# A hybrid retention and mLSTM backbone on one core: the first sixteen parameter blocks without splits, four latent chunks side by side

## The chip, the cores and the metric

The kernel runs on one core of a Trainium2 chip. TensorE (PE) multiplies matrices out of SBUF into PSUM; VectorE (DVE), ScalarE (ACT) and GpSimd (POOL) work beside it, each in the order of its own queue, and SyncE (SP) issues the transfers. The metric is the device time of one execution in microseconds (us).

## The reference

Two layers work on 512 latent tokens and 256 context tokens, with 1024 channels. What matters here is how a layer begins:

```python
mod_x = jax.nn.silu(c) @ w_ada[l] + b_ada[l]          # shift, scale, gate for the latent tokens
mod_c = jax.nn.silu(c_ctx) @ w_ada[l] + b_ada[l]      # the same for the context tokens
hx = _rmsnorm(x, norm_w) * (1.0 + sc_x[:, None]) + sh_x[:, None]
hc = _rmsnorm(ctx, norm_w) * (1.0 + sc_c) + sh_c
u = jnp.einsum('bld,de->ble', h, w_in) + b_in         # h is hx or hc
rq, rk, rv, rz, mq, mk, mv, mo, mz, mg, gr, gm = jnp.split(u, idx, axis=-1)
```

Behind it come a retention branch (`rq`, `rk`, `rv`, gate `rz`; rotary embedding on the latent q and k), an mLSTM branch (with the token gates `mg`), their merge, and one output projection with a residual. Everything is in 32-bit floats.

## The kernel before

**Layout.** Activations lie with channels on partitions, in 8 blocks `kb` of 128 channels; the 768 tokens are columns, context first (`CTX`, 256), then latent (`LAT`, 512). They form 6 chunks of 128 tokens: 0 and 1 are context, 2 to 5 latent. The modulated input is kept as a rounded part `h_hi` and its remainder `h_lo`; weights are split the same way by `split` (a copy on ACT, a subtraction on DVE or POOL) into `wh` and `wl`. A product is three matmuls: high by high, low by high, high by low.

**Who sets the order.** The code is written as one program; a scheduler places the instructions of each engine in a fixed order when the kernel is built, and buffers are taken from pools. A tile that takes a buffer waits until the last reader of the tile before it in that buffer is done. For the matmul results of the projections there are two PSUM buffers with the tag "lat" and two with the tag "ctx" (`atile`), in turn; small results use four others (`btile`). `stage` gives six SBUF buffers in turn.

**How it begins.** The first 16 of 24 parameter blocks of layer 0 are needed at once: block `kb` is the shift of channel block `kb`, block `8 + kb` its scale, each a 1024 by 128 matrix of 512 KB. `ada_load` and `ada_first` take the pair of a `kb` together: for kb 0 to 4 the pair is split, and 16 matmuls run with the silu values `sils` (both token kinds, high and low) as the stationary operand and the blocks as moving operand; for kb 5 to 7 (`NATSET`) the pair is used unsplit in fp32. `ada_fold` copies the resulting row and turns it into columns with small matmuls, and `mod_store` adds the bias. `rstd_rows` computes the norm (matmuls `ms_in`, `ms_inb`; for the context `ms_inc`, `ms_incb`). `modulate` scales and shifts each `kb`.

**The value and gate weights.** `projvg` multiplies one chunk of 128 tokens by 288 columns: 256 of `rv` for two heads and 32 of the token gates. `rvg(n)` calls it and then adds the bias twice on DVE: the values (L906) and the gate columns into `gtok`, a part of the gate work space `gw` (L907). Chunks 2 to 5 come first, then the first q projection (`ret_qk`, latent and context columns in one loop, L216 and L218), then chunks 0 and 1, then the k projection. Chunk n takes a buffer of the tag "lat" if n is even and "ctx" if it is odd. `gates` starts when `gtok` holds all six chunks; it is a long series on DVE. `rope` turns q and k on DVE (L649 to L651) and POOL. The context's modulation (`start_ctx`, on POOL, ACT and DVE: L389, L390) goes on beside `rvg` and the q projection.

## Time and profile before

| | us |
|---|---|
| median of 3 runs | 2023.96 (2020.58 to 2024.38) |
| the profiled execution, its own time | 2026.36 |
| its span, first to last instruction | 2024.6 |
| PE busy | 1986.7 (98% of the span) |
| DVE busy | 1347.0 (67%) |
| ACT busy | 715.9 (35%) |
| POOL busy | 371.0 (18%) |

The span is 1.8 us shorter than the profiled execution's own time, which is 2.4 us above the median. Mean granted TensorE clock over the span: 0.991 of full speed. A busy share is a mean over stages with different limits; what ends a wait is read from the stage itself.

### The profile page before, as it was taken

How to read it: one execution, taken by the hardware profiler on the slowest of the kernel's cores; microseconds unless marked ns; L12 is line 12 of the kernel's file. 1: busy time of each engine (PE TensorE's matmuls, PEld its weight loads, DVE VectorE, ACT ScalarE, POOL GpSimd, SP SyncE). 2: the span in 40 equal slices, each digit the busy share in tenths (PEclk: the TensorE clock that was granted, in tenths of full speed). 3: DMA queues.
4: the chain of work that ended last, by engine and by line, in shares of the span. 5: the costliest groups of instructions: out<-in, count | busy, mean ns of one | idle time of the engine just before them, and what ended most of it. 6: DMA issues, size and time to landing. Idle time of an engine off the chain costs nothing.

```text
span 2024.6 us, 32087 instructions
## 1 busy us (share of the span) xinstructions
PE 1986.7 (98%) x12612; PEld 1795.0 (89%) x12612; DVE 1347.0 (67%) x2897; ACT 715.9 (35%) x1346; POOL 371.0 (18%) x431
## 2 busy tenths in 40 slices
PE   7999999999999999999999998999999999999997
PEld 6988989999999999888888888899899999988887
DVE  7886785566868585766334689655568886763456
ACT  5423322333434334343112442322334444434323
POOL 4312221311212121100000332222212212110000
PEclk8989999999999999999999999999999999999999
DMA  8213432122323223456323521222233333325435
GB/s 298 75 50 100 137 98 87 58 88 74 112 74 110 80 87 115 160 205 213 119 79 144 162 86 59 95 62 74 89 114 99 116 118 116 118 94 190 133 122 170
DMA packets 80471, 231.64 MB, mean 114 GB/s; under 512 B 9600, under 2 KB 18048, under 8 KB 79296
## 3 DMA queue, kind: packets, MB, share of 16 engines
q1 hardware_dynamic: 76224, 213.66, 32.3%
q0 software_dynamic: 4096, 15.93, 2.0%
q8 instruction: 99, 1.62, 0.3%
q14 instruction: 52, 0.43, 0.1%
HBM read 208.39 MB, written 21.17 MB: 113 GB/s over the span
## 4 chain that ended last, share of the span: by engine, by line
PE 89%; DVE 6%; issue 2%; DMA 2%; ACT 0%; POOL 0%; SPq 0%; POOLq 0%; DVEq 0%
PE mv L232 11%; PE mqk_l L216 9%; PE rqk_l L216 8%; PE rv L232 4%; PE bm_l L216 4%; PE br_l L216 4%; PE gr_l L216 4%; PE gm_l L216 4%; PE mz_l L216 4%; PE rz_l L216 4%; PE mqk_c L218 3%; PE rqk_c L218 3%; PE ou L205 2%; PE ro L741 2%; PE mo L867 2%
## 5 line engine op out<-in xcount | busy, mean ns | idle before, releaser
L232 PE MATMUL mv<-wh_vo,h_hi 128*128 128x256 f32 x640 | 183.6, 287 | 0.0
L232 PE MATMUL mv<-wl_vo,h_hi 128*128 128x256 f32 x640 | 183.2, 286 | 0.0
L232 PE MATMUL mv<-wh_vo,h_lo 128*128 128x256 f32 x640 | 182.0, 284 | 0.0
L232 PEld LDWEIGHTS mv<-wh_vo,h_hi 128*128 128x128 f32 x640 | 122.6, 191 | 0.4
L232 PEld LDWEIGHTS mv<-wh_vo,h_lo 128*128 128x128 f32 x640 | 122.5, 191 | 0.2
L232 PEld LDWEIGHTS mv<-wl_vo,h_hi 128*128 128x128 f32 x640 | 122.4, 191 | 0.0
L790 DVE SCALAR_TENSOR_TENSOR cv<-u,vec,cv 128x770 f32<-128x770 f32 (+1 forms) x128 | 121.2, 948 | 1.8
L820 POOL TENSOR_TENSOR ws<-ws,gw 128x768 f32<-128x768 f32 (+1 forms) x32 | 53.4, 1688 | 321.9 <-PE mo L869 155.6
L216 PE MATMUL mqk_l<-h_lo,wh_mqk 128*128 128x512 f32 x256 | 103.8, 406 | 0.0
L216 PE MATMUL mqk_l<-h_hi,wh_mqk 128*128 128x512 f32 x256 | 103.3, 404 | 0.0
L216 PE MATMUL mqk_l<-h_hi,wl_mqk 128*128 128x512 f32 x256 | 102.6, 401 | 0.0
L652 POOL TENSOR_TENSOR ws<-ws,rp 128x512 f32<-128x512 f32 x32 | 52.9, 1653 | 176.6 <-DVE ws L651 144.8
L232 PE MATMUL rv<-wl_rv,h_hi 128*128 128x256 f32 x288 | 83.5, 290 | 0.0
L232 PE MATMUL rv<-wh_rv,h_hi 128*128 128x256 f32 x288 | 83.5, 290 | 0.0
L232 PE MATMUL rv<-wh_rv,h_lo 128*128 128x256 f32 x288 | 83.1, 289 | 0.0
L349 DVE SCALAR_TENSOR_TENSOR adj<-gw 128x512 f32<-128x512 f32 x112 | 74.9, 698 | 7.9 <-DMA gw<-in_wadat 4.2
L205 PE MATMUL ou<-yh,wl_wout 128*128 128x256 f32 (+1 forms) x256 | 79.3, 311 | 0.4 <-DVE wl_wout L162 0.4
L205 PE MATMUL ou<-yl,wh_wout 128*128 128x256 f32 (+1 forms) x256 | 79.1, 310 | 0.0
L205 PE MATMUL ou<-yh,wh_wout 128*128 128x256 f32 (+1 forms) x256 | 78.8, 310 | 0.0
L693 POOL TENSOR_TENSOR ws<-ws,ws 128x768 f32<-128x768 f32 (+1 forms) x32 | 52.9, 1673 | 118.8 <-PE ro L741 118.6
L741 PE MATMUL ro<-ws,ws 128*128 128x128 f32 x448 | 65.7, 279 | 7.7 <-DVE st L742 5.4
L741 PEld LDWEIGHTS ro<-ws,ws 128*128 128x128 f32 x448 | 60.1, 194 | 10.9 <-DVE st L742 6.1
(441 smaller groups left out, 6475.2 us busy)
## 6 DMA issues: line engine op xcount, KB each, us to landing
gw<-in_wadat SPq DMA_DIRECT2D x64, 256.0 KB, 3.5
raw_vo<-in_wblk SPq DMA_DIRECT2D x32, 512.0 KB, 4.0
raw_mqk<-in_wblk SPq DMA_DIRECT2D x32, 512.0 KB, 3.9
raw_wout<-in_wout SPq DMA_DIRECT2D x32, 512.0 KB, 3.6
gw<-grow SPq DMA_DIRECT2D x8, 1536.0 KB, 6.2
raw_qk<-in_wblk SPq DMA_DIRECT2D x16, 512.0 KB, 3.4
raw_zq<-in_wblk SPq DMA_DIRECT2D x16, 512.0 KB, 3.4
raw_kz<-in_wblk SPq DMA_DIRECT2D x16, 512.0 KB, 3.5
```

The costliest lines, as they stand in the source:

```text
L205: pe.matmul(dst, lw[:, j, kb], mv[:, kb, sl], start=first, stop=last)
L216: pe.matmul(lat, lw[:, j, kb], mv[:, kb, LAT], start=first, stop=last)
L218: pe.matmul(c[:, :NCTX], lw[:, j, kb], mv[:, kb, CTX], start=first, stop=last)
L232: pe.matmul(dst, sx[:, kb, tk], mv[:, :, kb], start=first, stop=last)
L349: v.scalar_tensor_tensor(junk, bufs[n % 4], 1.0, rows[:, d], op0=OP.mult, op1=OP.mult, accum_out=(part if q else m)[:, d:d + 1])
L652: g.tensor_tensor(dst[:, LAT], dst[:, LAT], t[:, :512], op=OP.add)
L693: g.tensor_tensor(chunks(qd[d][:, qsl], nq), chunks(qT[:, qsl], nq), xi[d][:, None, :].to_broadcast([P, nq, P]), op=OP.mult)
L741: pe.matmul(o, lt, rt, start=k == 0, stop=k == len(ops) - 1)
L790: v.scalar_tensor_tensor(y[:, o0:o0 + n], u[:, o0 + i:o0 + i + n], cw[i], y[:, o0:o0 + n], op0=OP.mult, op1=OP.add)
L820: g.tensor_tensor(qd[d][:, qsl], qT[:, qsl], gw[:, 2 + d, qsl], op=OP.mult)
L867: pe.matmul(o, ch(sT[d], n), vt[:, n, 0:129], start=True, stop=first)
```

## The change

The first sixteen blocks are no longer split. Shift blocks 1, 3, 4, 6 and 7 (`BYROW`) are loaded from the transposed copy of the parameters and multiplied on DVE by a row of silu values (`ada_shift`: two products of 512 columns with a running sum, then one small add), once for the latent tokens (d=0) and once for the context tokens (d=1). The other eleven blocks are the stationary operand of eight fp32 matmuls whose moving operand `sil` has two columns (`ada_first`), so that the result stands in columns at once. The rows of silu values are made by PE from the identity (`sil_row`) and lie in the start-up part of the gate work space `gw`. POOL scales `xin` by the norm in place, all eight `kb` before the first modulation. `projvg` takes several chunks and goes through them within each `kb`; for the latent ones the parameter and modulation steps of a `kb` are issued ahead of its matmuls (`start_lat`). The adds of `rvg` stand behind the matmuls of all four chunks. The first q and k projections do their latent columns one after the other, then come chunks 0 and 1, then the context columns of q and k. The weights for q and k are loaded in `start_lat`, no longer by `nextw`.

```diff
-        early = big.tile([P, 6, KB, P], F32, tag="b4", name="early")
+        xin = big.tile([P, KB, T], F32, tag="b2", name="xin")
+        shift = big.tile([P, 6, KB * P], F32, tag="b3", name="shift")
+        scale = big.tile([P, 6, KB, P], F32, tag="b4", name="scale")
         gw0 = gat.tile([P, 4, T], F32, tag="gw", name="gw_start").rearrange("p a b -> p (a b)").rearrange(
-            "p (a k c) -> p a k c", a=3, k=KB)
+            "p (a k) -> p a k", a=3)
+        srows, BYROW = gw0[:, 1:3], (1, 3, 4, 6, 7)
+        ring = [shift[:, 5]] + [scale[:, k].rearrange("p k c -> p (k c)") for k in range(6)] + [gw0[:, 0]]
+        ablk, acount = {}, [0]
 
         def ada_dma(kb):
-            r = []
-            for j, blk in enumerate((8 + kb, kb)):
-                k = (2 * kb + j) % 9
-                r.append(early[:, k] if k < 6 else gw0[:, k - 6])
-                nc.sync.dma_start(r[j], io["wada"][0, blk])
-            return r
-        raws = {0: ada_dma(0)}
-        xin = big.tile([P, KB, T], F32, tag="b2", name="xin")
+            for blk in (kb, 8 + kb):
+                if blk in BYROW:
+                    ablk[blk] = shift[:, BYROW.index(blk)]
+                    nc.sync.dma_start(ablk[blk], io["wadat"][0, blk])
+                else:
+                    ablk[blk] = ring[acount[0] % 8].rearrange("p (k c) -> p k c", k=KB)
+                    acount[0] += 1
+                    nc.sync.dma_start(ablk[blk], io["wada"][0, blk])
+        ada_dma(0)
         for kb in range(KB):
             nc.sync.dma_start(xin[:, kb, LAT], io["xT"][kb][:, LAT])
...
-        def projvg(w, hp, n, name):
-            ps = atile(("lat", "ctx")[n % 2], name)
...
+            pss = [atile(("lat", "ctx")[n % 2], f"{name}_{n}") for n in ns]
...
+                each(kb)
+                for ps, n in zip(pss, ns):
+                    for sx, mv in ((hp[0], w[0]), (hp[1], w[0]), (hp[0], w[1])):
+                        pe.matmul(ps[:, :VG], sx[:, kb, n * P:(n + 1) * P], mv[:, kb],
+                                  start=kb == 0 and sx is hp[0] and mv is w[0], stop=kb == KB - 1 and mv is w[1])
+            return pss
...
+        def sil_row(d):
+            for a in range(0, KB, 4):
+                ps = btile(f"silb{d}_{a}")
+                for k in range(4):
+                    pe.matmul(ch(ps, k), sil[:, a + k, d:d + 1].to_broadcast([P, P]), ident, start=True, stop=True)
+                s.activation(srows[:, d, a * P:(a + 4) * P], ps, AF.Copy)
+        spart = cst.tile([P, KB, 2, 2], F32, name="spart")
+        v.memset(spart, 0.0)
...
-        def ada_first(kb):
-            w = loaded["a", kb]
-            ps = btile(f"ada_{kb}")
-            if kb in NATSET:
-                for j in range(2):
-                    for k in range(KB):
-                        pe.matmul(ps[:, j * P:(j + 1) * P], sils[:, k].bitcast(F32), w[j][:, k], start=k == 0,
-                                  stop=k == KB - 1)
-            else:
-                for mv in w:
-                    for k in range(KB):
-                        pe.matmul(ps[:, :2 * P], sils[:, k], mv[:, :, k], start=k == 0 and mv is w[0],
-                                  stop=k == KB - 1 and mv is w[1])
-            return ps
-
-        def ada_fold(kb, ps):
-            row = stage(f"arow{kb}")[:4, :2 * P]
-            s.activation(row, ps[:4, :2 * P], AF.Copy)
-            pt = btile(f"adat_{kb}")
-            for j in range(2):
-                pe.matmul(pt[:, 2 * j:2 * j + 2], row[:, j * P:(j + 1) * P], fold, start=True, stop=True)
-            mod_store(0, 8 + kb, pt[:, 0:2])
-            mod_store(0, kb, pt[:, 2:4])
+        def ada_shift(kb, d):
+            junk, m = stage(f"adj0_{kb}_{d}"), mods[0][:, kb, d:d + 1]
+            for i in range(2):
+                w = ablk[kb][:, i * 512:(i + 1) * 512]
+                v.scalar_tensor_tensor(junk[:, :512], w, 1.0, srows[:, d, i * 512:(i + 1) * 512], op0=OP.mult, op1=OP.mult,
+                                       accum_out=spart[:, kb, d, i:i + 1])
+            v.scalar_tensor_tensor(m, spart[:, kb, d, 0:1], vec[0][:, V_BA + kb:V_BA + kb + 1], spart[:, kb, d, 1:2],
+                                   op0=OP.add, op1=OP.add)
+
+        def ada_first(blk):
+            ps = btile(f"ada_{blk}")
+            for k in range(KB):
+                pe.matmul(ps[:, 0:2], ablk[blk][:, k], sil[:, k], start=k == 0, stop=k == KB - 1)
+            mod_store(0, blk, ps[:, 0:2])
...
-        def modulate(l, x, rst, hp, sl, kb):
+        def modulate(l, x, rst, hp, sl, kb, scaled=False):
             m, d = mods[l], 1 if sl.start == 0 else 0
-            t = stage(f"xn{l}_{kb}_{d}")
-            g.tensor_tensor(t[:, sl], x[:, kb, sl], rst[:, sl], op=OP.mult)
+            if scaled:
+                t = x[:, kb]
+            else:
+                t = stage(f"xn{l}_{kb}_{d}")
+                g.tensor_tensor(t[:, sl], x[:, kb, sl], rst[:, sl], op=OP.mult)
...
-        ada_load(0)
-        rows = {0: ada_first(0)}
+        for kb in range(1, 4):
+            ada_dma(kb)
+        ada_first(0)
+        ada_first(8)
+        sil_row(0)
         for kb in range(KB):
             square_add(acc, xin[:, kb], kb, LAT)
-        ada_fold(0, rows[0])
-        ada_load(1)
         rstd_rows(acc, rst, LAT, "ms_in")
-        ada_load(2)
-        for kb in range(KB + 1):
-            if 0 < kb < KB:
-                rows[kb] = ada_first(kb)
-            ada_load(kb + 3)
-            if kb > 1:
-                ada_fold(kb - 1, rows[kb - 1])
-            if kb:
-                modulate(0, xin, rst, hp, LAT, kb - 1)
-            if kb == 3:
-                wload(0)
         for kb in range(KB):
-            nc.sync.dma_start(xin[:, kb, CTX], io["xT"][kb][:, CTX])
+            g.tensor_tensor(xin[:, kb, LAT], xin[:, kb, LAT], rst[:, LAT], op=OP.mult)
+
+        def start_lat():
+            for kb in range(KB):
+                if kb:
+                    if kb in BYROW:
+                        ada_shift(kb, 0)
+                    else:
+                        ada_first(kb)
+                    ada_first(8 + kb)
+                modulate(0, xin, rst, hp, LAT, kb, True)
+                if kb == 0:
+                    sil_row(1)
+                if kb + 4 < KB:
+                    ada_dma(kb + 4)
+                if kb == 3:
+                    wload(1)
+                    for k in range(KB):
+                        nc.sync.dma_start(xin[:, k, CTX], io["xT"][k][:, CTX])
+                yield
 
         def start_ctx():
             for kb in range(KB):
                 square_add(acc, xin[:, kb], kb, CTX)
             rstd_rows(acc, rst, CTX, "ms_inc")
             for kb in range(KB):
+                if kb in BYROW:
+                    ada_shift(kb, 1)
                 modulate(0, xin, rst, hp, CTX, kb)
                 if kb % 3 == 2:
                     yield
...
-            def ret_qk(w, blk, h, j):
+            def ret_qk(w, blk, h, j, only=None):
                 dst, vb, ctx = ((qTs[h % 2], V_RQ, need), (kTs[h % 2], V_RK, True))[j]
                 b = vc[:, vb + h:vb + h + 1]
-                pss = proj(w, blk, hp, ctx, f"rqk{l}_{h}_{j}")
-                rope(pss[0][0], b, dst, f"rp{l}_{h}_{j}")
-                if ctx:
-                    s.activation(dst[:, CTX], pss[1][0], AF.Identity, bias=b)
+                if only is None:
+                    pss = proj(w, blk, hp, ctx, f"rqk{l}_{h}_{j}")
+                elif only is CTX and not ctx:
+                    return
+                else:
+                    ps = atile("ctx" if only is CTX else "lat", f"rqk{l}_{h}_{j}_{only.start}")[:, :only.stop - only.start]
+                    mm3(ps, w[0], w[1], hp[0], hp[1], only, blk)
+                    pss = [(ps, only)]
+                for ps, sl in pss:
+                    if sl is LAT:
+                        rope(ps, b, dst, f"rp{l}_{h}_{j}")
+                    else:
+                        s.activation(dst[:, CTX], ps, AF.Identity, bias=b)
...
-            if l == 0:
-                late_consts()
             zet = sml.tile([P, 2, H], F32, tag="zet", bufs=1, name=f"zet{l}")
             rdec = sml.tile([P, 2, H], F32, tag="rdec", bufs=1, name=f"rdec{l}")
             for p in range(4):
                 bt = bias_row(p, f"rv{l}_{p}")
-                wv = nextw()
+                wv = nextw(l > 0 or p > 0)
...
-                    def rvg(n):
-                        ps = projvg(wv, hp, n, f"rvg{l}_{n}")
+                    def rvg(ps, n):
                         v.tensor_tensor(vt[:, n], ps[:, :2 * P], bt[:, :2 * P], op=OP.add)
                         v.tensor_tensor(ch(gtok, n).rearrange("p (a b) -> p a b", a=4)[:, :, 0:H],
                                         ps[:, 2 * P:VG].rearrange("p (a b) -> p a b", a=4),
                                         bt[:, 2 * P:VG].rearrange("p (a b) -> p a b", a=4), op=OP.add)
-                    for n in (2, 3, 4, 5):
-                        rvg(n)
-                        if n in (3, 5):
-                            tick()
+                    first = start_lat() if l == 0 else None
+                    for i, ps in enumerate(projvg(wv, hp, (2, 3, 4, 5), f"rvg{l}",
+                                                  (lambda kb: next(first)) if l == 0 else (lambda kb: kb % 3 or tick()))):
+                        rvg(ps, 2 + i)
+                    if l == 0:
+                        late_consts()
+                        main.append(start_ctx())
                     drain(main)
                     cosT, sinT = preg[:, 0:512], preg[:, 512:1024]
                     nc.sync.dma_start(cosT, io["rope"][0])
                     nc.sync.dma_start(sinT, io["rope"][1])
                     w = nextw(False)
-                    ret_qk(w, 0, 0, 0)
-                    rvg(0)
-                    rvg(1)
+                    for j in range(2):
+                        ret_qk(w, j, 0, j, LAT)
+                    for n, ps in enumerate(projvg(wv, hp, (0, 1), f"rvgc{l}")):
+                        rvg(ps, n)
+                    for j in range(2):
+                        ret_qk(w, j, 0, j, CTX)
```

How it stands on the engines. On DVE before, around the end of `rvg`: `rc_ms_inc` is the context's norm, L906 and L907 are the two adds for each of chunks 2 to 5, L685 scales values, and with L389 the context's modulation begins.

```order
L374 TENSOR_SCALAR rc_ms_inc<-ms_inc 128x2
L906 TENSOR_TENSOR ws_0_473<-rvg_2_577,br_rv_0_517 128x256
L907 TENSOR_TENSOR gw_475<-rvg_2_577,br_rv_0_517 128x4x8
L906 TENSOR_TENSOR ws_0_473<-rvg_3_604,br_rv_0_517 128x256
L907 TENSOR_TENSOR gw_475<-rvg_3_604,br_rv_0_517 128x4x8
L906 TENSOR_TENSOR ws_0_473<-rvg_4_646,br_rv_0_517 128x256
L907 TENSOR_TENSOR gw_475<-rvg_4_646,br_rv_0_517 128x4x8
L906 TENSOR_TENSOR ws_0_473<-rvg_5_673,br_rv_0_517 128x256
L907 TENSOR_TENSOR gw_475<-rvg_5_673,br_rv_0_517 128x4x8
L685 TENSOR_SCALAR ws_0_473<-ws_0_473,zet_515 128x3x128
L389 TENSOR_SCALAR xn_0_1_561<-xn_0_1_561,mod_116 128x256
```

The two adds of each chunk stand together here, ahead of the context's modulation.

On DVE after, from the same norm on: L295 are halves of `ada_shift`, here all for the context (the last digit in `adj_1_1`), L910 is the first of the two adds (L906 before), L377 begins the modulation.

```order
L359 TENSOR_SCALAR rc_ms_inc<-ms_inc 128x2
L295 SCALAR_TENSOR_TENSOR adj_1_1_598,spart<-shift,gw_start 128x512
L910 TENSOR_TENSOR ws_0_220<-rvg_2_269,br_rv_0_252 128x256
L295 SCALAR_TENSOR_TENSOR adj_3_1_612,spart<-shift,gw_start 128x512
L910 TENSOR_TENSOR ws_0_220<-rvg_3_270,br_rv_0_252 128x256
L295 SCALAR_TENSOR_TENSOR adj_1_1_598,spart<-shift,gw_start 128x512
L910 TENSOR_TENSOR ws_0_220<-rvg_4_271,br_rv_0_252 128x256
L910 TENSOR_TENSOR ws_0_220<-rvg_5_272,br_rv_0_252 128x256
L377 TENSOR_SCALAR xn_0_1_593<-xn_0_1_593,mod_113 128x256
```

The gate adds no longer stand behind the value adds. Of the rows that follow, seven more halves (L295), five small sums (L297), L692 (L685 before) and the modulation of seven of the eight `kb` (L377, L378) come next; this is their end, with L911, the second add (L907 before), and then the rope of q:

```order
L295 SCALAR_TENSOR_TENSOR adj_7_1_644,spart<-shift,gw_start 128x512
L297 SCALAR_TENSOR_TENSOR mod_113<-spart,vec_99 128x1
L377 TENSOR_SCALAR xn_6_1_639<-xn_6_1_639,mod_113 128x256
L378 TENSOR_TENSOR h_lo<-xn_6_1_639,h_hi 128x256
L911 TENSOR_TENSOR gw_222<-rvg_2_269,br_rv_0_252 128x4x8
L911 TENSOR_TENSOR gw_222<-rvg_3_270,br_rv_0_252 128x4x8
L911 TENSOR_TENSOR gw_222<-rvg_4_271,br_rv_0_252 128x4x8
L911 TENSOR_TENSOR gw_222<-rvg_5_272,br_rv_0_252 128x4x8
L377 TENSOR_SCALAR xn_7_1_648<-xn_7_1_648,mod_113 128x256
L378 TENSOR_TENSOR h_lo<-xn_7_1_648,h_hi 128x256
L647 SCALAR_TENSOR_TENSOR rp_0_0_680<-rqk_0_0_256_655,vec_99,ws_0_221 64x512
```

On PE before, the last matmuls of `rvg` for chunk 5, the norm of the context, and the first q projection; in brackets are the engines whose signals a row waits for.

```order
L239 MATMUL rvg_5_673<-wh_rvg_308,h_lo 128x288
L239 MATMUL rvg_5_673<-wl_rvg_309,h_hi 128x288
L378 MATMUL ms_incb<-k_ident,rc_ms_inc 128x128 [waits PE_49,Pool_49]
L378 MATMUL ms_incb<-k_ident,rc_ms_inc 128x128
L216 MATMUL rqk_0_0_l<-h_hi,wh_qk_0_519 128x512 [waits DVE_49,PE_49]
L216 MATMUL rqk_0_0_l<-h_lo,wh_qk_0_519 128x512
```

On PE after, the same place: `rqk_0_0_256` is the latent half of q and takes the buffer of `rvg_2`.

```order
L247 MATMUL rvg_4_271<-wh_rvg_254,h_lo 128x288
L247 MATMUL rvg_4_271<-wl_rvg_255,h_hi 128x288
L247 MATMUL rvg_5_272<-wh_rvg_254,h_lo 128x288
L247 MATMUL rvg_5_272<-wl_rvg_255,h_hi 128x288
L211 MATMUL rqk_0_0_256_655<-h_hi,wh_qk_0_389 128x512 [waits DVE_49,PE_49]
L211 MATMUL rqk_0_0_256_655<-h_lo,wh_qk_0_389 128x512
```

The norm has moved ahead of the last matmuls of `rvg`, and the projection has no context columns between. On POOL the clearing of `gtok` (L907 in the new file) now follows the scaling of the context and waits for DVE, since `gtok` and the rows of silu values that `ada_shift` reads lie in the same buffer `gw`.

## Rows read from the trace of the kernel before

**Rows 1.** The page: busy time and share of the span; the chain that ended last.

```profile
PE 1986.7 (98%) x12612; PEld 1795.0 (89%) x12612; DVE 1347.0 (67%) x2897; ACT 715.9 (35%) x1346; POOL 371.0 (18%) x431
...
PE 89%; DVE 6%; issue 2%; DMA 2%; ACT 0%; POOL 0%; SPq 0%; POOLq 0%; DVEq 0%
```

**Rows 2.** By stage: us, PE, PEld, DVE, ACT, POOL busy, TensorE clock, DMA share, GB/s.

```profile
25.00:61.58 36.58, 36.01 (x277) 34.17 (x277) 30.10 (x48) 16.18 (x32) 24.15 (x17) 1.00 0.59 202
61.58:85.47 23.89, 23.89 (x153) 21.79 (x152) 20.51 (x35) 11.43 (x22) 11.41 (x11) 1.00 0.19 56
85.47:132.80 47.33, 42.51 (x251) 37.38 (x249) 46.20 (x76) 12.73 (x23) 6.46 (x4) 0.94 0.16 54
132.80:153.00 20.20, 20.19 (x150) 20.19 (x151) 13.57 (x32) 4.47 (x8) 7.28 (x7) 0.88 0.22 71
```

**Rows 3.** Waits of PE from 76 to 153 us: total, times, longest.

```profile
PE ro L741 <- DVE st L742: 3.0, 1, 3.0
PE ro L741 <- DVE ws L701: 1.9, 1, 1.9
```

**Rows 4.** Timeline of DVE: start, duration, engine, line, operation, idle time before.

```profile
54.81 0.22 DVE L276 SCALAR_TENSOR_TENSOR mod<-adat,vec 128x2 f32<-128x2 f32 x1 [0.71 <-PE adat L317]
...
55.88 0.54 DVE L393 TENSOR_SCALAR xn<-xn,mod 128x512 f32<-128x512 f32 x1
...
60.49 0.42 DVE L906 TENSOR_TENSOR ws<-rvg,br_rv 128x256 f32<-128x256 f32 x1 [0.22 <-PE rvg L239]
60.83 0.18 DVE L907 TENSOR_TENSOR gw<-rvg,br_rv 128x32 f32<-128x32 f32 x1
...
62.24 0.48 DVE L685 TENSOR_SCALAR ws<-ws,zet 128x384 f32<-128x384 f32 x1
63.87 0.87 DVE L389 TENSOR_SCALAR xn<-xn,mod 128x256 f32<-128x256 f32 x1 [1.14 <-ACT h_hi L388]
...
71.30 0.75 DVE L390 TENSOR_TENSOR h_lo<-xn,h_hi 128x256 fp32r<-128x256 f32 x2
...
76.87 0.18 DVE L907 TENSOR_TENSOR gw<-rvg,br_rv 128x32 f32<-128x32 f32 x1
```

**Rows 5.** PE's groups, 24.9 to 61.5 us: busy us, mean ns, idle.

```profile
L303 PE MATMUL ada<-early,start_r 128*128 128x128 f32 x80 | 9.6, 278 | 0.0
...
L317 PE MATMUL adat<-fold,arow 4*128 4x2 f32 x28 | 4.2, 251 | 0.0
L308 PE MATMUL ada<-wl_ada,start_r 128*128 128x256 f32 x17 | 2.7, 296 | 0.4 <-DVE wl_ada L162 0.4
L308 PE MATMUL ada<-wh_ada,start_r 128*128 128x256 f32 x16 | 2.4, 295 | 0.0
L308 PE MATMUL ada<-start_r 128*128 128x256 f32 x16 | 2.2, 290 | 0.0
L303 PE MATMUL ada<-gw_start,start_r 128*128 128x128 f32 x16 | 1.9, 275 | 0.0
L372 PE MATMUL ms_inc<-ones_r,acc_in 128*128 128x1 f32 x4 | 0.6, 255 | 0.0
```

**Rows 6.** The page's costliest groups: the operation that ada_shift will use.

```profile
L349 DVE SCALAR_TENSOR_TENSOR adj<-gw 128x512 f32<-128x512 f32 x112 | 74.9, 698 | 7.9 <-DMA gw<-in_wadat 4.2
```

**Rows 7.** Timeline of POOL.

```profile
57.32 1.29 POOL L162 TENSOR_TENSOR h_lo<-xn,h_hi 128x512 fp32r<-128x512 f32 x1 [1.64 <-ACT h_hi L161]
```

**Rows 8.** The same columns for two shorter stretches.

```profile
19.60:24.90 5.30, 5.29 (x24) 5.29 (x25) 3.17 (x4) 2.85 (x4) 2.50 (x2) 0.50 1.03 411
132.80:137.00 4.20, 4.19 (x19) 4.19 (x20) 4.04 (x11) 0.21 (x1) 0.00 (x0) 0.50 0.37 124
```

**Rows 9.** The chain that ended last: start, us, what.

```profile
61.83 5.45 PE rqk_l L216 x24
...
69.42 0.71 PE rqk_c L218 x6
...
90.58 0.76 DVE rp L649
```

More of the change, by code (lines that the diff above doesn't have):

```diff
@@ L233, in projv, with projvg @@
             return ps
-        def projvg(w, hp, n, name):
-            ps = atile(("lat", "ctx")[n % 2], name)
+        def projvg(w, hp, ns, name, each=lambda kb: None):
+            pss = [atile(("lat", "ctx")[n % 2], f"{name}_{n}") for n in ns]
             for kb in range(KB):
-                for sx, mv in ((hp[0], w[0]), (hp[1], w[0]), (hp[0], w[1])):
-                    pe.matmul(ps[:, :VG], sx[:, kb, n * P:(n + 1) * P], mv[:, kb],
-                              start=kb == 0 and sx is hp[0] and mv is w[0], stop=kb == KB - 1 and mv is w[1])
-            return ps
+                each(kb)
[4 more added lines that the diff above has]
+            return pss
         sil = cst.tile([P, KB, 2], F32, name="sil")
@@ L247, in build @@
         v.tensor_scalar_mul(sil, sil, 0.5)
-        start_r = big.tile([P, 5, KB, P], F32R, tag="b3", name="start_r")
-        sils = start_r[:, 0]
-        v.memset(sils.bitcast(F32), 0.0)
-        s.activation(sils[:, :, 0:2], sil, AF.Copy)
-        v.tensor_tensor(sils[:, :, 2:4], sil, sils[:, :, 0:2].bitcast(F32), op=OP.subtract)
-        fold = cst.tile([4, 2], F32, name="fold")
-        v.tensor_tensor(fold, ident[:4, 0:2], ident[:4, 2:4], op=OP.add)
+        def sil_row(d):
[6 more added lines that the diff above has]
+        v.memset(spart, 0.0)
         mods, hvec = [], []
@@ L279, in mod_store @@
                 v.tensor_scalar(dst, src, b, 0.5, op0=OP.add, op1=OP.mult)
-        def ada_load(kb):
-            if kb >= KB:
-                return
-            raw = raws[kb] if kb in raws else ada_dma(kb)
-            if kb in NATSET:
-                loaded["a", kb] = raw
-                return
-            if kb % 3 == 2:
-                w = start_r[:, 1:3], start_r[:, 3:5]
-            else:
-                w = [wp.tile([P, KB * VG], F32R, tag=t, bufs=2, name=f"{t}_ada{kb}")[:, :2 * KB * P].rearrange(
-                    "p (j k c) -> p j k c", j=2, k=KB) for t in ("wh", "wl")]
-            for j in range(2):
-                split(w[0][:, j], w[1][:, j], raw[j])
-            loaded["a", kb] = w
@@ L297, in ada_first @@
-        def ada_first(kb):
-            w = loaded["a", kb]
-            ps = btile(f"ada_{kb}")
-            if kb in NATSET:
-                for j in range(2):
-                    for k in range(KB):
-                        pe.matmul(ps[:, j * P:(j + 1) * P], sils[:, k].bitcast(F32), w[j][:, k], start=k == 0,
-                                  stop=k == KB - 1)
-            else:
-                for mv in w:
-                    for k in range(KB):
-                        pe.matmul(ps[:, :2 * P], sils[:, k], mv[:, :, k], start=k == 0 and mv is w[0],
-                                  stop=k == KB - 1 and mv is w[1])
-            return ps
@@ L312, in ada_fold @@
-        def ada_fold(kb, ps):
-            row = stage(f"arow{kb}")[:4, :2 * P]
-            s.activation(row, ps[:4, :2 * P], AF.Copy)
-            pt = btile(f"adat_{kb}")
-            for j in range(2):
-                pe.matmul(pt[:, 2 * j:2 * j + 2], row[:, j * P:(j + 1) * P], fold, start=True, stop=True)
-            mod_store(0, 8 + kb, pt[:, 0:2])
-            mod_store(0, kb, pt[:, 2:4])
+        def ada_shift(kb, d):
[6 more added lines that the diff above has]
+                                   op0=OP.add, op1=OP.add)
@@ L461, in start_ctx @@
                     yield
-        main.append(start_ctx())
         late = {}
@@ L943, in build @@
                         w = nextw()
-                    if p == 0 and i == 0:
+                    if p == 0 and i < 2:
                         pass
```

## The prediction

> **What bounds the kernel now.** I read the page first: PE is busy 98% of the span, and the chain that ended last runs 89% over PE and 6% over DVE [rows 1]. So time is won only where PE gets less to do or waits less, and lost wherever PE waits anew. Then I read a table by stages [rows 2]. The change works in the first 85 us. From 25 to 61.58 PE is busy 36.01 of 36.58 us: it computes the parameter blocks and `rvg` of the four latent chunks. From 61.58 to 85.47 it is full (first retention projections, context chunks). From 85.47 to 132.80 it is not (42.51 of 47.33), and there DVE is (46.20); from 132.80 on PE is full again (20.19 of 20.20 us to 153). The list of waits [rows 3] says what ends the idle time: `ro` waits for DVE, for 3.0 us once and 1.9 us once. The chain up to 132.81 accordingly leaves PE at the last `rvg` of the context, near 77, and runs over DVE (gates, rope, splits) until `ro`. So two dates decide: when the retention projections begin (61.58), and when the gate pre-activations of the last context chunk are stored (76.87 + 0.18 = 77.05 [rows 4]), which starts that DVE stretch. What shifts both to later shifts the end, since behind 132.80 PE has no idle time to give back [rows 2].
>
> **The change, part by part.**
>
> *Parameter blocks on PE.* Between 24.9 and 61.5 PE gives them 9.6 us (80 matmul records), the same price for 16 further records (1.9), 2.7 + 2.4 + 2.2 for the split form and 4.2 for the transposes of `ada_fold` [rows 5]: 23.0 us. What replaces them in this stretch: nine blocks of 8 fp32 matmuls, each two records, as the 96 records of three pairs show (48 matmuls in the code), so 144; and 16 records of the second `sil_row`. A two-column moving operand isn't in the trace, but its neighbours are: 128 columns cost 9.6 / 80 = 0.12 us a record, one column (`ms_inc`) 0.6 / 4 = 0.15 [rows 5]. The narrow operand saves nothing then; the load of 128 stationary columns sets the price. 160 x 0.12 = 19.2 us, so PE wins 3.8 us. Bounds: 160 x 0.15 = 24 (a loss of 1.0) and, below, free matmuls (a gain of 23). I take 0.12, since the rows lie so close together.
>
> *Weighing a rule.* The Trainium skill ("TensorE: Matmul & The Clock Gate", section "Back-to-back issue gap") gives an isolated gap that shrinks with the moving columns, with a floor near 25 ns; by that 160 records would take an estimated 4 us and PE would win 19. The same section says that loads of the stationary operand set the pace too, and the 0.12 and 0.15 us above go that way. This is rival C below.
>
> *Splits, folds, silu rows, scaling.* Ten DVE splits, ten ACT copies and the `arow` copies vanish, `ada_shift` for d=0 comes in (10 halves of 0.70 [rows 6] = 7.0 us of DVE), and POOL scales `xin` ahead of time. All lies under PE's backlog before 61 (DVE is busy 30.10 of 36.58 [rows 2], and loses the splits). Uncovered it would be at most the net of these, some 1 to 2 us either way; I take nothing.
>
> *`rvg` of four chunks side by side.* The same 96 matmuls. But now each kb's matmuls follow that kb's modulation. For the last kb, from the parameter block's end to the split on POOL, the trace of before takes from 54.81 (store of the parameters), 55.88 (scaling on DVE) to 57.32 + 1.29 = 58.61 [rows 4, 7]: 3.8 us. In before the matmuls of other kbs stood behind it; now the order shows four `rvg` matmuls and `ms_inc` between, about 1 us. So of the 3.8 us won some 2.8 are given back, and `rvg` ends near 61.5 - 3.8 + 2.8 = 60.5. Bounds: 57.7 without that wait, 66 with three such waits.
>
> *The bank.* This is the term that decides. The latent projection `rqk` for q takes the PSUM buffer of `rvg_2` and waits until its last reader is done. In before that is the gate add L907, which stands right behind L906: done at 60.83 + 0.18 = 61.01, before PE got there [rows 4]. In after the gate adds (L911) stand on DVE behind almost all of the context's modulation, as the rows of the change show. DVE works in order, so from the moment `rvg_2` is complete it does first: 4 adds L910 of 0.42 = 1.7; 9 halves of `ada_shift` for d=1 of 0.70 = 6.3; 5 sums L297 (not in the trace; the nearest, the store of 54.81, is 0.22) = 1.1; the scaling L692 = 0.48; seven of eight kbs of modulation, where before took 63.87 to 71.30 + 0.75 = 72.05 for eight (16 operations, first and last in [rows 4]) = 8.18 x 7/8 = 7.2; and one L911, 0.18. Sum 17.0. Some of these start before the one ahead has wholly ended (L907 starts 0.34 after L906 of 0.42), so I take 16; bounds 14.5 (modulation at the rate of its last pair, 0.75 for two) and 17.0. `rvg_2` is complete some six matmuls before `rvg_5`, 0.8 us: 60.5 - 0.8 + 16 = 75.7. **Against 61.58 that is +14.1**, and PE has nothing else in its queue meanwhile: in-order behind `rqk` stand only more of `rqk` and `rvgc`.
>
> *The clock after the wait.* After PE's idle 3 us the granted clock is 0.50 (1.2 GHz) from 132.80 to 137.00 [rows 8]; half of 4.2 us is lost, 2.1. The wait here, 15 us, is longer. I add 2.1; bounds 0 and 4.
>
> *What follows.* In before the gate values were complete 77.05 - 61.58 = 15.5 us after the start of `rqk`. Now k's latent half comes before the context chunks (5.45 us [rows 9]) and q's context half behind them (24 matmuls at 0.71 / 6 = 0.12: 2.8 us [rows 9]): 15.5 + 5.45 - 2.8 = 18.1. So they are complete at 75.7 + 18.1 + 2.1 = 95.9, +18.9. From the DVE stretch behind it the rope of k is gone, three operations of 0.76 = 2.3 [rows 9], as it is done before: +16.6 at the `ro` of 132.81. PE's own work between is the same, so its path stands at 14.1 + 2.1 = +16.2. DVE still ends last. In layer 1 the edits only regroup the same matmuls, where no big wait stands; nothing, bounds -1 and +1.
>
> **Sum.** +16 us on the profiled execution's 2026.36 gives 2042. That execution lies 2.4 above the median of 2023.96; on the median: **2040 us**.
>
> **Rivals.**
>
> A, *the narrow matmuls don't raise the clock*. In before the granted clock is 0.50 (1.2 GHz) from 19.60 to 24.90, though PE was busy for all of it [rows 8]. If it stays there through the two-column stretches until `rvg` runs densely, some 64 records of them take 0.24 in place of 0.12, 7 to 8 us more: 2048. The Trainium skill (same page, "HAM oscillation — how this bites in real kernels") has the clock fall when PE idles between short bursts; the 0.50 behind the 3 us wait [rows 8] agrees.
>
> B, *the bank doesn't bind* (the other side). If DVE gets through its context block early, because most of it runs before `rvg_2` completes, `rqk` starts at rvg's end, 3.8 - 2.8 = 1 us or up to 3.8 us earlier than before; with the rope of k out of the DVE stretch the `ro` wait shrinks by 2.3: 2024 - 4 = 2020. It decides if less than 2 of the 16 us are left behind rvg_2. Against it: the second instruction of that block is an add that itself needs `rvg_2` complete, and all later ones are queued behind it. Nor could the gate adds be early by themselves: they write into `gw`, which POOL clears only when the last half of `ada_shift` for the context has read its silu row there.
>
> C, *narrow passes are cheap*. At 0.025 us a record PE wins 15 us more, but the loads of the blocks and the chain by kb take over (the DMA engines are busy 0.59 of the stretch to 61.58 [rows 2]); `rvg` would end near 50, `rqk` start near 65, +3.6; with the same steps behind it `ro` comes +6: 2030.
>
> D, *the DVE stretch takes it all up*: the splits and tables that stand in it (46.20 of 47.33 us busy) would be done while PE waits, so the end moves by less than 4. Against: DVE is itself busy during that wait, and the gates need the values that come last. 2024.
>
> **How the numbers follow.** Main case 0.70, own range 2034 to 2046 (rvg end 57.7 to about 63, queue 14.5 to 17.0, clock 0 to 2). A 0.11, B 0.08, C 0.06, D 0.05. A measurement of this kernel tells about 0.2%, 4 us. Faster is B without its upper edge, with some of D: 0.09; same the rest of D and the near edge of B and C: 0.06; slower 0.85. The range reaches into A above, 2049, and into C below, 2027.
>
> **What would show it.** In the profile after: PE idle 13 to 16 us between the last `rvg` of the latent chunks (near 60) and `rqk` (74 to 78), released by DVE L911; the granted clock 0.50 behind it; narrow ada records at 0.11 to 0.15 us apart; the last gate add near 96; `ro`'s wait for DVE ending near 149; the same PE work from there. The prediction falls if L911 of `rvg_2` is done within 3 us of the matmuls, or if records of two columns come 0.03 us apart or stay at 0.23.

## The result and the profile after

The changed kernel takes 2041.1 us (median of 4 runs, 2039.93 to 2041.92) against 2024.17 of the kernel before: a ratio of 1.0085 (95% interval 1.0073 to 1.0097), 17 us slower. The forecast was 2040 us. Its profiled execution took 2040.39 us, 14.0 more than that of before. Runs far above the rest (2396 us and more, two of them among the kernels below, at a granted clock of 0.75 and 0.76) are left out of all medians and ratios; one of them is the only profiled run of the kernel with 128 columns alone, so the clock is read from other kernels.

The page of the changed kernel: busy times, and the chain that ended last.

```profile
PE 1993.2 (98%) x12612; PEld 1804.7 (89%) x12612; DVE 1343.5 (66%) x2930; ACT 704.9 (35%) x1331; POOL 369.7 (18%) x431
...
PE 86%; DVE 8%; DMA 3%; issue 2%; ACT 1%; POOL 0%; SPq 0%; POOLq 0%; DVEq 0%; ACTq 0%
```

Against [rows 1] DVE's share of the chain has grown from 6 to 8%, PE's has fallen from 89 to 86%. Where, the list of PE's waits up to 170 us says:

```profile
PE rqk L211 <- DVE gw L911: 15.8, 1, 15.8
PE ada L303 <- DMA shift<-in_wada: 5.6, 1, 5.6
PE ro L748 <- DVE st L749: 2.3, 1, 2.3
```

The first line is the wait that the prediction placed there: the first q projection waits 15.8 us for the gate adds. The timeline of DVE in that stretch (start, duration, engine, line, operation, idle time before) shows the queue in front of them, from the value add of chunk 2 on:

```profile
64.25 0.42 DVE L910 TENSOR_TENSOR ws<-rvg,br_rv 128x256 f32<-128x256 f32 x1 [2.79 <-PE rvg L247]
64.59 1.13 DVE L295 SCALAR_TENSOR_TENSOR adj<-shift,gw_start 128x512 f32<-128x512 f32 x1
...
70.11 0.68 DVE L295 SCALAR_TENSOR_TENSOR adj<-shift,gw_start 128x512 f32<-128x512 f32 x1
...
80.17 0.43 DVE L378 TENSOR_TENSOR h_lo<-xn,h_hi 128x256 fp32r<-128x256 f32 x1
80.51 0.48 DVE L911 TENSOR_TENSOR gw<-rvg,br_rv 128x32 f32<-128x32 f32 x4
```

What the adds stand behind is POOL's clearing of `gw`, which waits for the last half that reads a silu row (the half starts at 78.50, for 0.68 us):

```profile
79.25 0.74 POOL L907 MEMSET gw<- 128x768 f32 x1 [2.03 <-DVE adj L295]
```

Grouped by line between 64.2 and 80.9 us, the dearest single part of DVE's queue is the context's halves of `ada_shift`; the two lines of the modulation together cost nearly as much:

```profile
L295 DVE SCALAR_TENSOR_TENSOR adj<-shift,gw_start 128x512 f32<-128x512 f32 x9 | 7.8, 867 | 0.0
L378 DVE TENSOR_TENSOR h_lo<-xn,h_hi 128x256 fp32r<-128x256 f32 x7 | 3.9, 563 | 0.0
L377 DVE TENSOR_SCALAR xn<-xn,mod 128x256 f32<-128x256 f32 x7 | 3.6, 515 | 0.0
```

And by stretches (us, PE, PEld, DVE, ACT, POOL busy, TensorE clock, DMA share, GB/s):

```profile
25.00:40.00 15.00, 15.00 (x74) 15.00 (x74) 14.68 (x22) 3.27 (x5) 12.66 (x8) 0.54 0.86 312
50.00:61.00 11.00, 11.00 (x63) 11.00 (x63) 3.88 (x10) 2.16 (x4) 4.12 (x4) 0.66 0.29 95
...
75.00:80.00 5.00, 0.00 (x0) 0.00 (x0) 4.96 (x14) 2.29 (x6) 1.61 (x3) 0.50 0.31 106
80.00:85.00 5.00, 4.16 (x10) 3.32 (x11) 1.70 (x8) 0.08 (x1) 0.00 (x0) 0.50 0.02 4
85.00:101.00 16.00, 16.00 (x88) 14.17 (x87) 4.64 (x7) 0.00 (x0) 2.58 (x2) 0.94 0.00 0
101.00:149.00 48.00, 48.00 (x309) 43.44 (x308) 43.21 (x64) 17.48 (x31) 8.44 (x5) 1.00 0.23 70
```

Three things are to be seen. PE stands idle from 65 to 80.84 while DVE is full. Before that, from 25 to 40, PE is busy for all 15 us, yet at a granted clock of 0.54 (mostly the lower level, 1.2 GHz); in before it was 1.00 from 25 on [rows 2]. And from 101 to 149 PE has no idle time, and just behind that only the wait of 2.3 us at `ro`, where before it was idle for 4.82 us up to `ro` [rows 2]: some of the loss is given back there.

### The profile page after: what moved, and what is told of

It is laid out like the page before. It is cut to its first block, busy times and chain, and to the rows that moved or that the text cites. A ratio compares the mean times of both kernels' runs of the same rounds, so it can differ in the third digit from the quotient of the medians.

```text
span 2038.6 us, 32088 instructions
## 1 busy us (share of the span) xinstructions
PE 1993.2 (98%) x12612; PEld 1804.7 (89%) x12612; DVE 1343.5 (66%) x2930; ACT 704.9 (35%) x1331; POOL 369.7 (18%) x431
## 4 chain that ended last, share of the span: by engine, by line
PE 86%; DVE 8%; DMA 3%; issue 2%; ACT 1%; POOL 0%; SPq 0%; POOLq 0%; DVEq 0%; ACTq 0%
PE mv L238 11%; PE mqk_l L222 9%; PE rqk_l L222 6%; PE bm_l L222 4%; PE br_l L222 4%; PE gr_l L222 4%; PE gm_l L222 4%; PE mz_l L222 4%; PE rv L238 4%; PE mqk_c L224 3%; PE rz_l L222 3%; PE rqk_c L224 2%; PE ro L748 2%; PE ou L211 2%; PE mo L874 2%
## 5 line engine op out<-in xcount | busy, mean ns | idle before, releaser
L749 DVE BATCH_NORM_STATS2 st<-ro 128x6 f32<-128x128 f32 x80 | 23.4, 292 | 67.0 <-PE ro L748 66.6
```

The costliest lines, as they stand in the source:

```text
L749: v.bn_stats(st6[:, i], o)
```

## The experiments

Nine of the ten kernels below start from the changed kernel, the last but one from the kernel before. Medians are in us; each ratio is to runs of the kernel before made in the same session (its medians: 2024.1 to 2025.1), so kernels of different sessions are compared by their ratios.

| kernel | median | ratio, 95% interval |
|---|---|---|
| gate adds early | 2031.86 | 1.0032 (1.0022 to 1.0043) |
| all blocks on PE | 2041.62 | 1.0079 (1.0062 to 1.0097) |
| 128 moving columns | 2033.75 | 1.0042 (1.0027 to 1.0057) |
| gate adds early, 128 columns | 2023.42 | 0.9995 (0.9986 to 1.0004) |
| context halves early | 2027.33 | 1.0013 (1.0004 to 1.0022) |
| context halves early, 128 columns | 2020.83 | 0.9983 (0.9974 to 0.9993) |
| the same, two blocks by rows | 2016.15 | 0.9959 (0.9947 to 0.9972) |
| the same, k behind the context chunks | 2019.47 | 0.9981 (0.9972 to 0.9990) |
| before, layer 1 in the new order | 2022.55 | 0.9990 (0.9981 to 1.0000) |
| after, layer 1 in the old order | 2042.98 | 1.0085 (1.0072 to 1.0099) |

**The bank: gate adds early.** The gate columns of chunks 2 to 5 go into unused columns of a work buffer; ACT copies them later (not printed here).

```diff
 def rvg(ps, n):
     v.tensor_tensor(vt[:, n], ps[:, :2 * P], bt[:, :2 * P], op=OP.add)
+    o = 5958 + 4 * H * (n - 2)
+    if l == 0 and n > 1:
+        v.tensor_tensor(ws2[:, o:o + 4 * H], ps[:, 2 * P:VG], bt[:, 2 * P:VG], op=OP.add)
+        return
...
```

> The changed kernel, but the gate columns of the four latent chunks are added into a small buffer of their own right behind the value adds, and copied into the gate work space later by ACT; the same is computed. Theory 1 (the bank: q's projection waits for the gate adds, which stand behind the context's modulation): PE's wait of 15.8 us before the first q projection falls below 1.5 us, q starts at 65 to 67 in place of 80.84, the first rz projection at 92 to 95 in place of 107.4, and the time falls by 11 to 15 us, to 2026 to 2030. Rival (the loss is the half clock on the narrow parameter matmuls, the wait only hides it): the wait goes, but the time falls by less than 5 us, to 2036 or more.

Waits of PE to 170 us and two stretches of this kernel:

```profile
PE ro L748 <- DVE st L749: 5.7, 1, 5.7
PE ada L303 <- DMA shift<-in_wada: 5.3, 1, 5.3
PE ms_inb L363 <- POOL rc_ms_in L360: 1.8, 1, 1.8
PE rvgc L247 <- DVE ws L649: 1.5, 1, 1.5
```

```profile
25.00:40.00 15.00, 15.00 (x78) 15.00 (x79) 14.68 (x20) 4.36 (x7) 12.71 (x8) 0.56 0.88 316
...
50.00:61.00 11.00, 11.00 (x67) 11.00 (x67) 4.39 (x10) 1.89 (x3) 4.07 (x3) 0.69 0.30 95
```

The wait for the gate adds is gone; q starts at 65.2, as `rvg` ends, and the first `rz` projection at 91.2 in place of 107.4. By the ratios the time falls by 0.53%, some 10.7 us, just under the 11 to 15 expected (the median of 2031.86 lies above the 2026 to 2030 expected): part of the gain meets a longer wait of `ro` for DVE (5.7 in place of 2.3 us). The bank is shown as the largest part of the loss. The clock from 25 to 61 is as it was.

**The width: 128 moving columns.** The two columns are repeated, so that each of the eleven blocks' matmuls moves 128.

```diff
-pe.matmul(ps[:, 0:2], ablk[blk][:, k], sil[:, k], start=k == 0, stop=k == KB - 1)
+pe.matmul(ps[:, 0:P].rearrange("p (a b) -> p a b", b=2), ablk[blk][:, k],
+          sil[:, k].unsqueeze(1).to_broadcast([P, P // 2, 2]), start=k == 0, stop=k == KB - 1)
```

> The changed kernel, but the moving operand of the eleven blocks' matmuls is 128 columns (the two columns repeated 64 times) in place of 2; the same is computed. If the narrow operand is why the granted clock is 0.55 between 25 and 40 us though PE is busy throughout: the granted clock there rises to 0.9 or more, the records keep their 0.11 us at full clock, the latent value projection ends at 59 to 61 in place of 64.85, and with the wait for the gate adds unchanged the time falls by 3 to 5 us, to 2036 to 2038. Rival (the clock there stands for another reason, for instance the idle time before): the clock stays near 0.55 and the time stays at 2041 or rises.

By the ratios the time fell by 0.43%, 8.7 us, more than the 3 to 5 expected, though the intervals of the two ratios leave room for 5. The clock is read from the next kernel, which has the same edit on top of the early gate adds.

> Both single edits together: gate columns into a small buffer right behind the value adds, and 128 moving columns in place of 2; the same is computed. It shows the clock in a kernel without the wait. If narrow operands set the clock: granted clock over 0.9 from 25 to 61 us (0.56 and 0.69 with narrow ones), the latent value projection ends at 58 to 61, the first q projection starts within 1.5 us behind it, and the time falls by 4 to 8 us against the early gate adds alone, to 2023 to 2028. If the clock stands for another reason: still near 0.56, time 2031 or more.

Stretches of it, and its group of parameter matmuls:

```profile
25.00:40.00 15.00, 14.02 (x119) 13.60 (x117) 14.78 (x19) 4.85 (x8) 13.23 (x9) 1.00 0.90 318
...
50.00:61.00 11.00, 9.52 (x61) 8.29 (x60) 8.21 (x20) 4.12 (x7) 8.21 (x7) 1.00 0.27 95
```

```profile
L303 PE MATMUL ada<-sil,scale 128*128 128x128 f32 x112 | 13.2, 276 | 0.0
```

The granted clock is 1.00 where it was 0.56 and 0.69, `rvg` ends at 58.4 in place of 65.3, and the time falls by another 0.37%, 7.5 us, within the 4 to 8 expected. The two edits together bring the ratio from 1.0085 to 0.9995: the wait and the clock together are as large as the whole loss. 112 records take 13.2 us with 128 columns; with 2 columns in the changed kernel the same group took 18.8 us:

```profile
L303 PE MATMUL ada<-sil,scale 128*128 128x2 f32 x112 | 18.8, 298 | 0.0
```

So the wider matmul is the cheaper one here, 0.118 us a record in place of 0.168: not because of its own work, but by the clock. Where the clock was up in the changed kernel, 16 narrow records (57.45 to 59.15 us) stood 0.11 us apart too.

**All blocks on PE.** No `ada_shift`, no silu rows, a ring of twelve buffers outside the gate work space.

```diff
-srows, BYROW = gw0[:, 1:3], (1, 3, 4, 6, 7)
...
-                    if kb in BYROW:
-                        ada_shift(kb, 0)
-                    else:
-                        ada_first(kb)
+                    ada_first(kb)
```

> The changed kernel with all sixteen blocks as stationary operands, no block by DVE rows, no silu rows; the same is computed. Theory 1: without the nine to ten halves of the context on DVE and without silu rows in the gate work space the wait before q falls from 15.8 to under 10 us; five more blocks of 16 records at 0.11 to 0.22 us put the end of the latent value projection 9 to 18 us later (minus 3 to 6 for the silu rows), near 70 to 77. Time 2036 to 2044, near the changed kernel. Rival (the DVE rows are cheap and the wait is set by something else): the wait stays at 14 us or more and the time rises by 8 or more.

```profile
61.00:75.00 14.00, 14.00 (x68) 14.00 (x68) 1.20 (x4) 0.63 (x1) 2.52 (x2) 0.52 0.00 1
75.00:80.00 5.00, 4.22 (x20) 4.14 (x20) 0.90 (x3) 0.63 (x1) 1.94 (x2) 0.50 0.00 0
```

The wait falls not just under 10 us but to nothing (q starts at 82.1, as `rvg` ends), and `rvg` ends near 82, later than the 70 to 77 expected: PE is busy with narrow matmuls at the lower clock. One loss has taken the place of the other, at the same total time. What held the gate adds, DVE's load or the shared buffer, this kernel leaves open, since it removes both.

**The shared buffer: context halves early.** DVE does the context's halves right behind the latent ones, and PE makes both rows of silu values at the start.

```diff
+sil_row(1)
...
 if kb in BYROW:
-    ada_shift(kb, 0)
+    for d in range(2):
+        ada_shift(kb, d)
...
-                if kb in BYROW:
-                    ada_shift(kb, 1)
```

> The changed kernel, but the context halves of the five blocks by DVE rows are done right behind the latent halves (in the loop over the latent blocks), so that the silu rows are read before the value projection ends; the moving operand stays narrow; the same is computed. Theory 1 in its second part (the gate adds are late because the gate work space can't be cleared before the silu rows are read): the gate adds stand behind the value adds again, the wait of 15.8 us falls below 1.5 us, q starts at 65 to 69, time 2028 to 2033. Rival (the gate adds are late only because the order is so written): the wait stays above 8 us.

Waits of PE to 170 us, the clearing of `gw` on POOL, the first two adds on DVE, and one stretch:

```profile
PE ada L303 <- DMA shift<-in_wada: 5.3, 1, 5.3
PE ro L746 <- DVE st L747: 2.5, 2, 2.0
...
PE rvg L247 <- ACT h_hi L167: 1.3, 1, 1.3
```

```profile
53.09 0.74 POOL L905 MEMSET gw<- 128x768 f32 x1 [3.76 <-PE ada L303]
```

```profile
69.78 0.42 DVE L908 TENSOR_TENSOR ws<-rvg,br_rv 128x256 f32<-128x256 f32 x1 [3.25 <-PE rvg L247]
70.12 0.18 DVE L909 TENSOR_TENSOR gw<-rvg,br_rv 128x32 f32<-128x32 f32 x1
```

```profile
25.00:40.00 15.00, 15.00 (x71) 15.00 (x72) 13.75 (x18) 2.76 (x4) 12.09 (x9) 0.50 0.92 331
```

`gw` is cleared at 53.09 in place of 79.25, the first gate add stands right behind its value add, and the wait is gone, though nothing was done to the gate adds themselves and DVE has the same operations to do. So it was the silu rows in `gw`, read late, that kept the adds late. q starts at 70.4, later than the 65 to 69 expected: the context's halves now lie on DVE ahead of the latent modulation, and the clock is 0.50 from 25 to 40. The time is 2027.33, just under the range. With 128 columns:

> The same with 128 moving columns; differs from the run before in that alone. Narrow operands set the clock: granted clock over 0.9 from 25 to 61 us, q starts at 61 to 63, 3 to 6 us less than the run before: 2022 to 2027. Otherwise the same time as it.

```profile
25.00:40.00 15.00, 10.63 (x79) 10.45 (x79) 15.00 (x20) 4.09 (x6) 12.30 (x9) 0.88 0.92 336
...
50.00:61.00 11.00, 10.20 (x75) 9.79 (x73) 10.43 (x32) 5.57 (x12) 3.02 (x3) 0.89 0.14 48
```

6.5 us less than the narrow one (3 to 6 expected), and below the kernel before; the clock is 0.88 and 0.89, just under the 0.9 expected, and q starts at 65.4, later than the 61 to 63 expected. DVE is busy for all 15 us from 25 to 40, while PE is not: now DVE's rows seem to hold the start, which the next kernel asks.

**Fewer rows on DVE.** Only blocks 3 and 7 stay there.

```diff
-srows, BYROW = gw0[:, 1:3], (1, 3, 4, 6, 7)
+srows, BYROW = gw0[:, 1:3], (3, 7)
...
```

> The same as the run before, with only shift blocks 3 and 7 by DVE rows and the other fourteen as stationary operands with 128 moving columns; the same is computed. If, with the bank and the clock out of the way, the modulation that waits behind the DVE rows is what holds the value projection: it ends near 57 to 59, q starts near 58 to 60, and the kernel runs below both, at 2016 to 2021. If PE's work is what holds it (three more blocks of 1.8 us): 2024 to 2030.

2016.15 us, the fastest of all, 8.6 us below the kernel before and 4.7 below the last one. Against the last one the reason expected holds: `rvg` ends at 61.8 in place of 65.4, the first `rz` projection starts 3.6 us earlier (85.5 against 89.1) and the first `mv` 4.1 (384.1 against 388.2). Only the size is off, 61.8 and not 57 to 59. Against the kernel before, though, `rz` starts at the same time and the first `mv` 4.7 us ahead: what is gained on it up to there isn't won in the parameter part but between the two. The next kernel asks where, with the old order of the first q and k.

```diff
-for j in range(2):
-    ret_qk(w, j, 0, j, LAT)
+if l == 0:
+    ret_qk(w, 0, 0, 0)
...
```

> The last kernel (two blocks by rows, 128 moving columns), but with the order of the kernel before for the first layer's first q and k: q with both kinds of columns, the two context chunks, then k in its old place; the same is computed. In the last kernel the first gate projection starts as in before (-0.02 us), and yet it is 5.2 us ahead of it at 158 us. If that comes from k's projection and rope standing ahead of the gates' DVE stretch: here the gain at 158 us falls to 0 to 2 us and the time rises by 3 to 5 us, to 2019 to 2021. Rival (it comes from the parameter part or the earlier splits): the time stays within 1 us of 2016.

The waits of PE on DVE before `ro`, first in the kernel with k ahead, then in the one with k behind the context chunks:

```profile
PE ro L747 <- DVE st L748: 2.5, 2, 2.0
```

```profile
PE ro L747 <- DVE st L748: 5.4, 1, 5.4
```

The time rises by 3.3 us, as expected, and the wait of `ro` by 2.9. From the first `rz` to the first `mv` the kernel before takes 303.3 us, the one with k ahead 298.6, the one with k behind 302.2: so 3.6 of the 4.7 us that are gained there go with the order of k. At `mv` itself the two kernels differ by 1.8 only (their profiled executions by 2.1), because with k behind `rz` starts 1.8 us earlier. That lies ahead of what the edit touches: from 35 to 40 us the granted clock was 1.00 there and 0.66 in the kernel with k ahead.

**The layer boundary.** Before with the new order in layer 1 alone, and after with the old order there (`projvg` chunk by chunk, q with both kinds of columns, k in its old place). Of the first of the two, a part:

```diff
+if l == 0:
+    for n in (2, 3, 4, 5):
+        rvg(projvg(wv, hp, (n,), f"rvg{l}")[0], n)
...
+else:
+    for i, ps in enumerate(projvg(wv, hp, (2, 3, 4, 5), f"rvg{l}", lambda kb: kb % 3 or tick())):
+        rvg(ps, 2 + i)
...
```

> The kernel before, with the new order of value chunks and of the first q and k projections in layer 1 alone; the same is computed. If the 2.4 us that the changed kernel regains at the layer boundary come from that order: 2021 to 2022, 2 to 3 us under the kernel before, and the listed waits of PE around 1140 to 1200 (2.3 us for the split on DVE, 2.2 for the table) shrink. Rival (they come from the shifted start of the first layer, by chance of where stalls fall): no difference within 1 us.

> The changed kernel with layer 1 in the old order (value chunks one after the other, q with both kinds of columns, k in its old place); the same is computed. If the changed kernel regains 2.4 us at the layer boundary by the new order there: 2 to 3 us slower than it, 2043 to 2044, and its lag at the end of the trace is 17 to 18 us in place of 14.5. Rival (it is regained by other shifts): the same 2041.

Two markers, `gm_l` late in layer 0 and `mvc` in layer 1, in before, after, before with the new order, and after with the old one (quantiles of the durations in ns, then first and last start in us of what the window holds):

```profile
L216 PE MATMUL gm_l<-h_hi,wh_gm x18: 391/392/475, 806.5 to 828.7; 128*128 128x512 f32 x18
...
L232 PE MATMUL mvc<-wh_mv,h_hi x16: 277/283/288, 1492.4 to 1498.0; 128*128 128x256 f32 x16
```

```profile
L222 PE MATMUL gm_l<-h_hi,wh_gm x6: 392/395/474, 823.9 to 829.1; 128*128 128x512 f32 x6
...
L238 PE MATMUL mvc<-wh_mv,h_hi x7: 277/283/288, 1507.3 to 1509.7; 128*128 128x256 f32 x7
```

```profile
L216 PE MATMUL gm_l<-h_hi,wh_gm x19: 391/392/475, 805.7 to 829.5; 128*128 128x512 f32 x19
...
L232 PE MATMUL mvc<-wh_mv,h_hi x16: 277/283/288, 1490.6 to 1496.2; 128*128 128x256 f32 x16
```

```profile
L222 PE MATMUL gm_l<-h_hi,wh_gm x5: 392/395/474, 824.8 to 829.1; 128*128 128x512 f32 x5
...
L238 PE MATMUL mvc<-wh_mv,h_hi x12: 277/283/287, 1510.7 to 1514.9; 128*128 128x256 f32 x12
```

Between the markers lie 685.9 us in before, 683.4 in after, 684.9 in before with the new order, 685.9 in after with the old one. That would fit the new order as what brings the 2.5 us to after, though it brings before only 1.0 at this place and some 2 in all (ratio 0.9990, at the edge of what is told from no change). But it isn't shown. The other kernels of the list have the new order in layer 1 too: in six of them the same stretch takes 682.8 to 684.7 us, but in the context halves early with 128 columns 685.9 (805.2 to 1491.1), as in the old order, and each of these figures is of a single execution. In time, after with the old order is 1.9 us above after, with the same ratio of 1.0085: it can't be told there either.

## Why the prediction was right

The cause was right: q waits for the gate adds, for about as long as forecast. The time came out as near as it did partly by luck: some terms were off, and their errors took each other away.

- *Parameter blocks on PE, 0.12 us a record.* Mis-sized: 0.168 on the mean of 112 records, because the clock stayed at 0.54 from 25 to 40; 30 records from 29.78 to 36.04 us stood 0.21 apart, close to the 0.23 named as a sign against the forecast. Rival A, given 0.11, came true in part. With the chain of the last kb, `rvg` ended at 65.0 in place of 60.5, 4.5 us later (A had priced 7 to 8), inside the term's bounds but beyond the 63 of the own range. That a record's price hardly depends on the moving columns was right where the clock was up, 0.11 us with 2 columns and 0.118 with 128; that the load of the stationary operand sets it fits this and wasn't tested apart. Rival C (cheap narrow passes) is refuted: even the quickest block, the 16 records from 57.45 us, has them 0.11 us apart.
- *The bank.* Right in place and size: from the value add of chunk 2 (64.25) to the start of q (80.84) 16.6 us, forecast 16. Inside it the halves cost 7.8 us in place of 6.3, and the modulation 7.5 in place of 7.2. The lower bound of 14.5 doesn't come out of its rows: with 0.75 us for two operations of the modulation the sum of 17.0 falls to 15.05, and with the same 1 us off to 14. Early gate adds alone took 10.7 us off, and the early context halves showed why the adds were late. Rival B is refuted by the 15.8 us.
- *The clock after the wait.* Forecast 2.1 us. The chain lists 14.03 us for the 48 matmuls of q and k against 2 x 5.45 [rows 9], 3.1 lost; the granted clock was 0.50 from 75 to 85.
- *What follows.* The gate values were complete at 101.64 + 0.18 = 101.82, +24.8 against 77.05 (forecast +18.9). But `ro` came at 151.76 in the chain, +18.95 against the 132.81 of before (forecast +16.6): the DVE stretch shrank by 5.8 us, not 2.3. The rope of k, 2.3, is one part. The other is a pair of scalings that the forecast had not looked at. In before they ran beside POOL's L693:

```profile
76.98 2.13 DVE L683 TENSOR_SCALAR ws<-ws,zet 128x640 f32<-128x640 f32 x1
79.04 1.79 DVE L684 TENSOR_SCALAR ws<-ws,zet 128x256 f32<-128x256 f32 x1
```

```profile
76.86 3.83 POOL L693 TENSOR_TENSOR ws<-ws,ws 128x768 f32<-128x768 f32 x2
```

In after POOL's two operations come at 104.76, behind them:

```profile
101.75 0.62 DVE L690 TENSOR_SCALAR ws<-ws,zet 128x640 f32<-128x640 f32 x1
102.29 0.34 DVE L691 TENSOR_SCALAR ws<-ws,zet 128x256 f32<-128x256 f32 x1
```

That is 3.92 - 0.96 = 3.0 us. Together with the rope 5.3 of the 5.8. In the two kernels of the q and k order the same pair takes 0.62 and 0.34 with k ahead, 1.00 and 1.80 with k behind, where POOL's pair runs beside it (74.14 to 77.98). That POOL's operations stretch DVE's is what these rows agree on; no kernel moved POOL's pair alone, so it's argued, not shown.
- *Layer 1.* Forecast nothing within 1 us; measured -2.5 between the markers. Outside the bounds, small in the sum, and not shown to come from the order.
- *The sum.* In profiled times +14.0 (forecast +16). The lag was 24.8 us at the gate values (5.9 above the forecast: 4.5 at `rvg`, the rest in the queue, the clock and the context chunks), 18.95 at `ro`, 18.1 at the first `mv` (406.9 against 388.8), 17.4 at `gm_l`, 14.9 at `mvc` in layer 1. So what was late at first and what was given back later about cancelled. With the relief of 2.3 us that the forecast had, the 24.8 us would have led to +22.5, an estimate of 2046.5 on the median, beyond the own range of 2034 to 2046. By medians it's +17. Rival D, that the DVE stretch takes it all up, was wrong in degree: it gave back 5.8 of 24.8 us.

## What to carry to other kernels

Before a consumer is moved behind other work on its engine, look for who waits on the buffer that it reads last; here a 0.18 us add held a PSUM buffer for 16 us, and it couldn't be moved forward while its own target lay in a space that was still read for something else. Where matmuls get a much narrower moving operand, read the granted clock of that stretch and not the busy share alone: here 128 columns in place of 2 were worth 6 to 9 us in three pairs of kernels. And when the start of a stage moves, look at what it no longer, or newly, runs beside: here a neighbour on POOL seems to have been worth as much (3.0 us) as the work that was taken away (2.3).

## What the runs showed of the hardware

- PE busy for 15.00 of 15 us, in the changed kernel some 10 of them with fp32 matmuls of 2 moving columns, ran at a granted clock of 0.54 (0.56 and 0.50 in two other kernels); with 128 columns of the same values in their place it was 1.00 and 0.88, and 112 records took 13.2 us in place of 18.8. The Trainium skill ("TensorE: Matmul & The Clock Gate", section "What's actually happening") says that the clock follows how busy the PE has been; the listed busy time alone doesn't tell that here, where the stretches at the lower clock are those with more of it (15.00 against 14.02 and 10.63 us).
- A DVE product with running sum of 128x512 took 0.68 us alone. Of the changed kernel's halves for the context, those that began while POOL was scaling the context took 1.13 to 1.21 (at 64.59, 71.91 and 76.56 us) and 0.86 (at 65.99). Two that began 0.03 us ahead of POOL's scaling (70.11 and 73.83) still took 0.68, and there it was POOL's operation that took 1.24, in place of the 0.83 and 0.78 beside the halves of 71.91 and 76.56. Each product is followed by a read of the accumulator, listed at 0.07 or 0.08 us.
